# A decoder step with single-neuron experts: both f16 parts of a gate weight in one matmul of 256 columns for 88 of 256 tokens

## The chip, the cores and the metric

The kernel runs on one core of a Trainium2 chip. The metric is the device time of one execution in microseconds (us). Five engines work side by side, each through its own queue in order: TensorE (PE, with its weight loads shown apart as PEld), VectorE (DVE), ScalarE (ACT), GpSimd (POOL) and SyncE (SP). DMA transfers are started from the queues of SP, ACT and POOL.

## What is computed

The reference is one decoder layer for 256 prompt tokens and 64 sample tokens with a model width of 2048: attention and a gating unit, then a PEER layer, then a per-layer embedding. Only the PEER layer matters here. For each token it scores 128 + 128 keys in 8 heads, takes the best 16 pairs of each head, and so names 8 x 16 = 128 experts out of 128 x 128 = 16384, each a single neuron:

```python
v1, i1 = lax.top_k(s1, PEER_TOPK)
v2, i2 = lax.top_k(s2, PEER_TOPK)
sc, ci = lax.top_k(cand, PEER_TOPK)      # cand: all sums of v1 and v2
e = take(i1, ci // PEER_TOPK) * N_KEYS + take(i2, ci % PEER_TOPK)
```

The token's result is the sum over its 128 experts e of g(e) * gelu(x . u(e)) * v(e), where g is the softmax of the scores within a head, and u and v are the experts' rows.

## The kernel before

For the 256 prompt tokens the kernel does not gather rows of experts. It computes all 16384 experts densely, and multiplies each hidden value by a gate that is zero where the expert was not chosen. An expert's number is (row, column) in a 128 x 128 grid. The dense work is cut into 128 hidden units of 128 experts: `u_unit(e)` multiplies the unit's weights with the tokens (three passes for F32R precision, L94 to L96 in `mm3`, 48 matmuls of 256 columns into the PSUM tile `ps_mm`), and ACT applies gelu (L647). Each weight tile comes by an SP DMA as f32 and is split in halves: ACT makes the high part `w_hi` (L77), DVE the low part `w_lo` (L78), in a ring of four buffers. Later units (L639, L640) use 512 and 256 columns. `v_group(g)` then takes eight units at a time, and sums over them into `ps_o` (again L94 to L96), from where DVE adds to the residual `hT` (L813), 256 times in all.

The gates are built between units 14 and 28 by `g_batch(tb)`, sixteen calls of sixteen tokens, each in two halves of NB = 8 tokens. For a half, DVE makes with f16 tiles of 128 partitions (the token's 128 choices) and 1024 columns: `e1` and `e2`, the one-hot rows and columns of the choices (L704), and `p1`, `p2`, which are `e1` times the high and the low f16 part of the gate weight (L706). The weight is scaled by WSC = 16384 ahead of the split. The columns lie as 128 keys x 4 tokens, so one token's 128 columns have a stride of four elements. For each token PE multiplies `e2` (as the weights) by `p1` and by `p2`, both accumulated into the same 128 columns of a PSUM tile `ps_s` (L711): this gives the token's 128 x 128 grid of gates. Four tokens (a quad) fill one tile; there are two buffers of it. ACT copies the quad with the scale 1/WSC into `g_st` (L715), in which a token's values lie with a stride of 16 f32 elements. After 16 tokens a POOL DMA writes `g_st` to the DRAM matrix `gd` (L721).

`weights(g)` reads a group's gates back by an ACT DMA (`g_t`, L782), DVE multiplies the hidden values by them (L786), and ACT and DVE split the product (`wh` L114, `wl` L117) for `v_group`. The first group cannot start before the last batch of gates has gone through `gd`.

The order on each engine is not written by hand here: a scheduler interleaves the batches with the units ahead of time, and the queues then run in that order. Before the change a batch stands on PE as sixteen f16 matmuls, 7 of a hidden unit, sixteen f16 matmuls, 41 of hidden units.

Of the kernel before, what the change touches and what calls it, by code (L numbers as in the profile page):

```python
# [15 lines left out]
F16 = mybir.dt.float16  # L16
AF = mybir.ActivationFunctionType
ALU = mybir.AluOpType
AX = mybir.AxisListType

P = 128
D = 2048
NC_ = D // P
TP = 256
# [15 lines left out]
WSC = 16384.0  # L40
# [8 lines left out]
def _build(ctx, tc, nc, a):  # L49
    vec, act, pool, pe = nc.vector, nc.scalar, nc.gpsimd, nc.tensor  # L50
# [15 lines left out]
    def psum(tag, cols, parts=P):  # L66
        t = ps.tile([P, 512], F32, tag=tag, name="ps_" + tag)
        return t[:parts, :cols]
# [18 lines left out]
    def unit(src, lo_eng=None):  # L87
        r = raw.tile([P, 16, P], F32, name="w_raw")
        nc.sync.dma_start(r.rearrange("p a b -> p (a b)"), src)
        return split(r, lo_eng)  # L90

    def mm3(out, w, xh, xl, start, stop):
        wh, wl = w
        pe.matmul(out, wh, xh, start=start, stop=False)  # L94
        pe.matmul(out, wh, xl, start=False, stop=False)  # L95
        pe.matmul(out, wl, xh, start=False, stop=stop)  # L96
# [58 lines left out]
    hT = cp.tile([P, NC_, T], F32, name="hT")  # L155
# [108 lines left out]
    for b4 in range(2):  # L264
        pt = psum("tr", 512)
# [188 lines left out]
    for h in range(SH):  # L454
        tok = toks[h]
        for i in range(3):
            n = P if i < 2 else TS
# [6 lines left out]
        for sl, n, b in ((slice(0, TP), 2, bias[:, h]), (slice(TP, T), DB, bias[:, h, 0:DS])):  # L464
# [5 lines left out]
                op0=ALU.mult, op1=ALU.add,  # L470
# [20 lines left out]
    with tc.tile_pool(name="wo", bufs=2, reuse_waits="tile") as wo:  # L491

        early = [psum(tag, T) for tag in ("mm", "mm", "o", "o")]
        for half in range(2):
            for o2 in range(2):
                w = unit(a["w_out"][2 * half + o2])
                for k in range(2):
                    for c in range(8):
                        i = 8 * half + c
                        mm3(early[2 * o2 + k], w(8 * k + c), *xmix(i), i == 0, i == NC_ - 1)  # L500
        for o in range(NC_):
            xr = wo.tile([P, T], F32, name="xr", bufs=4)
            pool.dma_start(xr, a["xT"][o])
            if o < 4:
                pt = early[o]
            else:
                pt = psum("mm", T)
# [100 lines left out]
    for n, h in enumerate((0, 4, 1, 5, 2, 6, 3, 7)):  # L608
        sp = [psum("s", 256), psum("tr", 256), psum("o", 256)]
        r0 = 64 * (h // 4)  # L610
        for half in range(2):
            pt = psum("mm", T)
            dense(pt, unit(a["wq"][2 * h + half]), xh)
            q = rt.tile([P, T], F32, name="q_t", bufs=2)
# [5 lines left out]
        for i in range(2):  # L620
# [3 lines left out]
            scale=rcol[r0 : r0 + 64, 2:3],  # L624
# [5 lines left out]
    def u_unit(e, halves):  # L630

        t = up.tile([P, TP], F32, name="act", bufs=LEAD)
        w = unit(a["uT"][e])
        x = lambda c: (A0 if c < 8 else C)[2][:, c % 8, :, 0:TP]
        if halves:
            pt = psum("mm", 2 * TP).rearrange("p (a t) -> p a t", a=2)
            for c in range(NC_):
                wh, wl = w(c)
                pe.matmul(pt, wh, x(c), start=c == 0, stop=False)  # L639
                pe.matmul(pt[:, 0], wl, x(c)[:, 0], start=False, stop=c == NC_ - 1)  # L640
            act.activation(t, pt[:, 1], AF.Copy)
            vec.tensor_add(t, t, pt[:, 0])
        else:
            pt = psum("mm", TP)
            for c in range(NC_):
                mm3(pt, w(c), x(c)[:, 0], x(c)[:, 1], c == 0, c == NC_ - 1)
        act.activation(t, t if halves else pt, AF.Gelu_apprx_tanh)  # L647
        acts[e] = t
# [33 lines left out]
    NB = 8  # L682
    with tc.tile_pool(name="oh", bufs=2, side="right", reuse_waits="tile") as ohp:
        i4 = ohp.tile([P, NK, 4], F16, name="i4", bufs=1)
        vec.tensor_copy(i4, i128.unsqueeze(2).to_broadcast([P, NK, 4]))

        small = [ohp.tile([P, 4, P], F16, name=f"sel{i}", bufs=1) for i in range(2)]
        for tp, b in zip(picks, small):
            act.activation(b[:, 0:2], tp[:, 0 : 2 * P].rearrange("p (a b) -> p a b", a=2), AF.Copy)
            act.activation(b[:, 2], tp[:, 2 * P :], AF.Copy, scale=WSC)  # L690
            vec.scalar_tensor_tensor(b[:, 3], tp[:, 2 * P :], WSC, b[:, 2], op0=ALU.mult, op1=ALU.subtract)

        def g_batch(tb):
            st = ohp.tile([P, NK, 16], F32, name="g_st")
            for hb in range(16 // NB):
                t0 = tb * 16 + hb * NB
                t1 = t0 % P
                shape = [P, NB // 4, NK, 4]
                of = lambda k: (
                    small[t0 // P][:, k, t1 : t1 + NB].rearrange("p (q t) -> p q t", t=4).unsqueeze(2).to_broadcast(shape)  # L700
                )
                e1, e2, *parts = [ohp.tile(shape, F16, name=n) for n in ("e1", "e2", "p1", "p2")]
                for k, e in enumerate((e1, e2)):
                    vec.tensor_tensor(e, i4.unsqueeze(1).to_broadcast(shape), of(k), op=ALU.is_equal)  # L704
                for k, p in enumerate(parts):
                    vec.tensor_mul(p, e1, of(2 + k))  # L706
                for q in range(NB // 4):
                    gp = psum("s", 512)
                    for t in range(4):
                        for k, p in enumerate(parts):  # L710
                            pe.matmul(  # L711
                                gp[:, t * P : t * P + P], e2[:, q, :, t], p[:, q, :, t], start=k == 0, stop=k == 1
                            )
                    b = hb * NB + 4 * q
                    act.activation(  # L715
                        st[:, :, b : b + 4].rearrange("p a t -> p t a"),
                        gp.rearrange("p (t a) -> p t a", t=4),
                        AF.Copy,
                        scale=1.0 / WSC,
                    )  # L720
            pool.dma_start(  # L721
                gd[:, :, tb * P : tb * P + P].rearrange("g p x -> p g x"),
                st.rearrange("p (g i) t -> p g (i t)", g=NG),
            )


        for c4 in range(4):
            tp = psum("tr", 512)
            for c in range(4 * c4, 4 * c4 + 4):
                xd = ohp.tile([P, 2, TS], F32, name="xd", bufs=4)  # L730
                act.activation(
                    xd, hT[:, c, TP:].unsqueeze(1).to_broadcast([P, 2, TS]), AF.Copy, scale=g_ffn[:, c : c + 1]
                )
                pe.transpose(tp[:, c % 4 * P : c % 4 * P + P], xd.rearrange("p a b -> p (a b)"), ident)
            act.activation(xc[:, c4 * 512 : c4 * 512 + 512], tp, AF.Copy)

        tb = 0
        for e in range(AHEAD, U1):
            u_unit(e, False)
            while tb < 16 and tb * (U1 - AHEAD) < 16 * (e - AHEAD + 1):  # L740
                g_batch(tb)
                tb += 1
# [32 lines left out]
    def paced():  # L775
        state["unit"] += 1
        while state["n"] < min(128, state["unit"] * 128 // N_UNITS):
            c_step()
# [15 lines left out]
    def add_samples():  # L794
        for c4 in range(2):
            pt = psum("tr", 512)
            for c in range(8):
                dt = 8 * c4 + c
                pe.matmul(pt[:, c * TS : c * TS + TS], acc[:, dt * P : dt * P + P], stack, start=True, stop=True)
            vec.tensor_add(  # L800
                hT[:, 8 * c4 : 8 * c4 + 8, TP:], hT[:, 8 * c4 : 8 * c4 + 8, TP:],
                pt.rearrange("p (c t) -> p c t", c=8),
            )

    def v_group(g, ws):
        for d2 in range(8):
            w = unit(a["v_t"][g, d2])
            for k in range(2):
                pt = psum("o", TP)
                for i in range(GRP):  # L810
                    mm3(pt, w(8 * k + i), *ws[i], i == 0, i == GRP - 1)
                dt = 2 * d2 + k
                vec.tensor_add(hT[:, dt, 0:TP], hT[:, dt, 0:TP], pt)  # L813
            paced()
            if g == NG - 1 and d2 == 1:
                add_samples()
# [6 lines left out]
    for g in range(NG):  # L823
        v_group(g, ws)
        if g + 1 < NG:
            upto = LEAD + (NK - LEAD) * (g + 1) // (NG - 1)
            while done < upto:
                if done == upto - 1 and upto < NK:
                    ws = weights(g + 1)
                u_unit(done, True)  # L830
                paced()
                done += 1
            if upto == NK:
                ws = weights(g + 1)
# [5 lines left out]
    with tc.tile_pool(name="pl", bufs=2, reuse_waits="tile") as pl:  # L840
# [5 lines left out]
        for o in range(NC_):  # L846
            if o % 8 == 0:
                w_ple = unit(a["ple_w"][o // 8])
            pp = psum("s", T)
# [9 lines left out]
        for o in range(NC_):  # L859
            pt = psum("mm", T)  # L860
# [130 lines left out]
```

## Time and profile before

| | us |
|---|---|
| median of 3 runs | 2167.61 |
| lowest and highest run | 2167.24, 2169.64 |
| the profiled execution | 2168.27 |
| its span in the profile | 2166.5 |
| PE busy in the span | 2151.7 (99%) |
| DVE busy | 1699.5 (78%) |
| ACT busy | 1034.0 (48%) |
| POOL busy | 254.8 (12%) |

The span is the time from the first to the last instruction that the profile holds; the profiled execution took 1.8 us more. Records of matmuls overlap, since they are pipelined: what one costs on PE is the distance from its start to the next one's, not its duration.

### The profile page before, as it was taken

What the parts mean: (1) busy time and instruction counts of PE and PEld (TensorE: products, weight loads), DVE (VectorE), ACT (ScalarE), POOL (GpSimd) and SP (SyncE); (2) the same over time, 40 slices, a digit from 0 to 9 for tenths busy, and PEclk for the clock granted to TensorE, in tenths of its full rate; (3) what the DMA queues carried; (4) which work ended last, traced back from release to release, by engine and by line L of the source; (5) the groups of instructions that cost most, each with busy time, mean ns of one, the idle gap of its engine ahead of it and who ended that gap; (6) DMA issues with size and microseconds to landing.
All of it is one profiled execution on the core that took longest, in us unless ns stands there. A gap on an engine that the chain in (4) does not pass through costs nothing.

```text
span 2166.5 us, 38217 instructions
## 1 busy us (share of the span) xinstructions
PE 2151.7 (99%) x15552; PEld 2040.7 (94%) x15552; DVE 1699.5 (78%) x2808; ACT 1034.0 (48%) x1544; POOL 254.8 (12%) x190
## 2 busy tenths in 40 slices
PE   8999999999999999999999999999999999999999
PEld 7879999999999999999999999999999999999998
DVE  6674875799988688788878888788888888788754
ACT  5346454335476644444444444444444444445632
POOL 2000000000001111111111111111212221111000
PEclk9999999999999999999999999999999999999999
DMA  7412354343567788888788878889888888887452
GB/s 278 142 59 99 121 187 162 134 137 137 173 197 235 223 322 328 307 315 315 296 321 316 306 291 317 305 311 330 292 311 310 309 312 317 297 317 250 169 180 83
DMA packets 80575, 531.39 MB, mean 245 GB/s; under 512 B 9126, under 2 KB 13654, under 8 KB 19584
## 3 DMA queue, kind: packets, MB, share of 16 engines
q1 hardware_dynamic: 49936, 349.76, 45.3%
q0 software_dynamic: 24912, 158.30, 19.7%
q10 hardware_dynamic: 5552, 20.91, 2.6%
q8 instruction: 122, 2.00, 0.4%
q14 instruction: 53, 0.43, 0.1%
HBM read 509.07 MB, written 20.84 MB: 245 GB/s over the span
## 4 chain that ended last, share of the span: by engine, by line
PE 90%; issue 5%; DVE 2%; DMA 1%; ACT 1%; POOL 1%; ACTq 0%; SPq 0%; POOLq 0%; DVEq 0%
PE ps_mm L639 16%; PE ps_o L94 11%; PE ps_o L96 11%; PE ps_o L95 11%; PE ps_mm L95 9%; PE ps_mm L94 9%; PE ps_mm L96 8%; PE ps_mm L640 8%; PE ps_s L711 1%; POOL gd L721 1%; DVE w_lo L78 1%; DMA hT<-in_xT 0%; DMA g_t<-gd 0%; PE ps_s L94 0%; PE ps_s L96 0%
## 5 line engine op out<-in xcount | busy, mean ns | idle before, releaser
L77 ACT ACTIVATE w_hi<-w_raw 128x1024 fp32r<-128x1024 f32 x662 | 700.8, 1059 | 921.9 <-PE ps_o L95 340.2
L78 DVE TENSOR_TENSOR w_lo<-w_raw,w_hi 128x1024 fp32r<-128x1024 f32 x662 | 805.9, 1222 | 249.0 <-ACT w_hi L77 244.9
L94 PE MATMUL ps_o<-wh,w_hi 128*128 128x256 f32 x2048 | 575.5, 281 | 0.8 <-ACT wh L114 0.8
L95 PE MATMUL ps_o<-wl,w_hi 128*128 128x256 f32 x2048 | 573.3, 280 | 1.0 <-DVE wl L117 1.0
L96 PE MATMUL ps_o<-wh,w_lo 128*128 128x256 f32 x2048 | 569.9, 278 | 0.3 <-DVE w_lo L78 0.3
L95 PEld LDWEIGHTS ps_o<-wl,w_hi 128*128 128x128 f32 x2048 | 385.0, 188 | 1.4 <-DVE wl L117 1.4
L94 PEld LDWEIGHTS ps_o<-wh,w_hi 128*128 128x128 f32 x2048 | 384.4, 188 | 1.8 <-ACT wh L114 1.2
L96 PEld LDWEIGHTS ps_o<-wh,w_lo 128*128 128x128 f32 x2048 | 385.0, 188 | 0.5 <-DVE w_lo L78 0.5
L95 PE MATMUL ps_mm<-a,w_hi 128*128 128x320 f32 (+1 forms) x1008 | 310.5, 308 | 1.2 <-DVE a L119 1.2
L94 PE MATMUL ps_mm<-a,w_hi 128*128 128x320 f32 (+1 forms) x1008 | 308.7, 306 | 1.5 <-ACT w_hi L187 1.1
L96 PE MATMUL ps_mm<-a,w_lo 128*128 128x320 f32 (+1 forms) x1008 | 306.8, 304 | 0.5 <-DVE w_lo L78 0.3
L639 PE MATMUL ps_mm<-a,w_hi 128*128 128x512 f32 x768 | 270.9, 392 | 0.0
L639 PE MATMUL ps_mm<-c,w_hi 128*128 128x512 f32 x768 | 270.8, 391 | 0.0
L640 PE MATMUL ps_mm<-c,w_lo 128*128 128x256 f32 x768 | 215.1, 280 | 0.0
L640 PE MATMUL ps_mm<-a,w_lo 128*128 128x256 f32 x768 | 215.1, 280 | 0.0
L95 PEld LDWEIGHTS ps_mm<-a,w_hi 128*128 128x128 f32 x1008 | 190.5, 189 | 9.0 <-issue 6.6
L94 PEld LDWEIGHTS ps_mm<-a,w_hi 128*128 128x128 f32 x1008 | 190.3, 189 | 8.2 <-issue 4.9
L96 PEld LDWEIGHTS ps_mm<-a,w_lo 128*128 128x128 f32 x1008 | 190.3, 189 | 4.4 <-issue 3.2
L639 PEld LDWEIGHTS ps_mm<-c,w_hi 128*128 128x128 f32 x768 | 143.7, 187 | 31.8
L639 PEld LDWEIGHTS ps_mm<-a,w_hi 128*128 128x128 f32 x768 | 143.7, 187 | 31.3
L757 POOL DMA_INDIRECT row<-in_v_rows,c_e x64 | 111.3, 1739 | 496.2 <-DVE xc L770 444.6
L757 POOL DMA_INDIRECT row<-in_u_rows,c_e x64 | 100.7, 1573 | 510.7 <-DVE row L762 504.5
(343 smaller groups left out, 3145.3 us busy)
## 6 DMA issues: line engine op xcount, KB each, us to landing
w_raw<-in_uT SPq DMA_DIRECT2D x128, 1024.0 KB, 5.0
w_raw<-in_v_t SPq DMA_DIRECT2D x128, 1024.0 KB, 6.6
w_raw<-in_w_in SPq DMA_DIRECT2D x25, 1024.0 KB, 4.9
w_raw<-in_w_out SPq DMA_DIRECT2D x16, 1024.0 KB, 4.8
w_raw<-in_wq SPq DMA_DIRECT2D x16, 1024.0 KB, 4.8
gd<-g_st POOLq DMA_DIRECT2D x16, 1024.0 KB, 6.3
g_t<-gd ACTq DMA_DIRECT2D x16, 1024.0 KB, 6.2
w_raw<-in_w_gate SPq DMA_DIRECT2D x16, 1024.0 KB, 5.0
```

The costliest lines, as they stand in the source:

```text
L77: last = act.activation(hi, s, AF.Copy)
L78: (lo_eng or vec).tensor_sub(lo, s, hi.bitcast(F32))
L94: pe.matmul(out, wh, xh, start=start, stop=False)
L95: pe.matmul(out, wh, xl, start=False, stop=False)
L96: pe.matmul(out, wl, xh, start=False, stop=stop)
L639: pe.matmul(pt, wh, x(c), start=c == 0, stop=False)
L640: pe.matmul(pt[:, 0], wl, x(c)[:, 0], start=False, stop=c == NC_ - 1)
L711: pe.matmul(gp[:, t * P : t * P + P], e2[:, q, :, t], p[:, q, :, t], start=k == 0, stop=k == 1)
L721: pool.dma_start(gd[:, :, tb * P : tb * P + P].rearrange("g p x -> p g x"), st.rearrange("p (g i) t -> p g (i t)", g=NG),)
L757: pool.indirect_dma_start(out=row, out_offset=None, in_=tab, in_offset=bass.IndirectOffsetOnAxis(ap=c_e[:, j : j + 1], axis=0),)
```

## The change

`p1` and `p2` become the two halves of one tile `pp`. A quad is made in a new way when its number (4 * tb + b // 4) is a multiple of three: 22 of the 64 quads, 88 of the 256 tokens. For two such tokens one `ps_s` tile is taken, and for each token one matmul of 256 columns (128 for each part) fills half of it (L715 of the changed kernel). ACT copies the high parts' 128 x 2 x 128 values to `g_st` (L717), and DVE adds the low parts' from PSUM onto them there (L718). The other quads are made as before (L723, L726), without the scale. 1/WSC is applied later instead: the 256 additions into `hT` become `scalar_tensor_tensor` instructions (L823).

On PE this takes away 88 matmuls and 88 weight loads, and 88 of the remaining ones have 256 columns. ACT has 42 copies of 128 x 512 and 44 of 128 x 2 x 128 in place of 64 of 128 x 512. DVE has 44 additions more. The numbers of instructions on POOL and SP are the same.

```diff
-                e1, e2, *parts = [ohp.tile(shape, F16, name=n) for n in ("e1", "e2", "p1", "p2")]
+                e1, e2 = [ohp.tile(shape, F16, name=n) for n in ("e1", "e2")]
+                pp = ohp.tile([P, 2] + shape[1:], F16, name="pp")
...
-                for k, p in enumerate(parts):
-                    vec.tensor_mul(p, e1, of(2 + k))
+                for k in range(2):
+                    vec.tensor_mul(pp[:, k], e1, of(2 + k))
                 for q in range(NB // 4):
+                    b = hb * NB + 4 * q
+                    if (4 * tb + b // 4) % 3 == 0:
+
+                        for t in range(0, 4, 2):
+                            gp = psum("s", 512).rearrange("p (t k a) -> p t k a", t=2, k=2)
+                            for i in range(2):
+                                pe.matmul(gp[:, i], e2[:, q, :, t + i], pp[:, :, q, :, t + i], start=True, stop=True)
+                            o = st[:, :, b + t : b + t + 2].rearrange("p a t -> p t a")
+                            act.activation(o, gp[:, :, 0], AF.Copy)
+                            vec.tensor_add(o, o, gp[:, :, 1])
+                        continue
                     gp = psum("s", 512)
                     for t in range(4):
-                        for k, p in enumerate(parts):
+                        for k in range(2):
                             pe.matmul(
-                                gp[:, t * P : t * P + P], e2[:, q, :, t], p[:, q, :, t], start=k == 0, stop=k == 1
+                                gp[:, t * P : t * P + P], e2[:, q, :, t], pp[:, k, q, :, t], start=k == 0, stop=k == 1
                             )
...
                         AF.Copy,
-                        scale=1.0 / WSC,
                     )
...
-                vec.tensor_add(hT[:, dt, 0:TP], hT[:, dt, 0:TP], pt)
+                vec.scalar_tensor_tensor(
+                    hT[:, dt, 0:TP], pt, 1.0 / WSC, hT[:, dt, 0:TP], op0=ALU.mult, op1=ALU.add
+                )
```

The scheduler's order changes with it. After the change a pattern of three batches (twelve quads) repeats. In the order of PE, with "a" to "k" for the four fast quads a, c, g, j and the eight slow ones b1, b2, d1, d2, h1, i1, k1, k2, and "F n" for n matmuls of hidden units, it reads: F 35, a, F 14, b1, b2, F 2, c1, F 2, c2, F 29, d1, d2, F 6, g1, F 2, g2, F 5, h1, F 37, i1, j1, F 5, j2, F 7, k1, k2. A fast quad's two pairs are c1 and c2.

PE before, the end of a half-batch in the middle of the stage (`e_...` is the column one-hot as weights, `p_...` the two products, `a_78` the tokens' high or low part):

```order
L711 LDWEIGHTS e_8003
L711 MATMUL ps_s<-p_8004,e_8003 128x128
L711 LDWEIGHTS e_8003
L711 MATMUL ps_s<-p_8005,e_8003 128x128
L95 MATMUL ps_mm<-a_78,w_hi 128x256
L96 MATMUL ps_mm<-a_78,w_lo 128x256
L94 MATMUL ps_mm<-a_78,w_hi 128x256
```

PE after, at such a place, the quad b2's end and the fast quad c:

```order
L723 LDWEIGHTS e_7978
L723 MATMUL ps_s<-pp,e_7978 128x128
L94 MATMUL ps_mm<-a_78,w_hi 128x256
L95 MATMUL ps_mm<-a_78,w_hi 128x256
L715 LDWEIGHTS e_7978
L715 MATMUL ps_s<-pp,e_7978 128x256
L715 LDWEIGHTS e_7978
L715 MATMUL ps_s<-pp,e_7978 128x256
L96 MATMUL ps_mm<-a_78,w_lo 128x256
L94 MATMUL ps_mm<-a_78,w_hi 128x256
L715 LDWEIGHTS e_7978
L715 MATMUL ps_s<-pp,e_7978 128x256
```

The run of sixteen f16 matmuls is broken up: behind b2 two matmuls of a hidden unit, the first pair, two more, the second pair.

DVE before, one batch between two splits of weight halves:

```order
L78 TENSOR_TENSOR w_lo<-w_raw,w_hi 128x1024 x2
L704 TENSOR_TENSOR e_7975<-i_6479,sel_6482 128x1024
L706 TENSOR_TENSOR p_7976<-e_7974,sel_6482 128x1024
L706 TENSOR_TENSOR p_7977<-e_7974,sel_6482 128x1024
L704 TENSOR_TENSOR e_8003<-i_6479,sel_6482 128x1024
L706 TENSOR_TENSOR p_8004<-e_8002,sel_6482 128x1024
L706 TENSOR_TENSOR p_8005<-e_8002,sel_6482 128x1024
L704 TENSOR_TENSOR e_8093<-i_6479,sel_6482 128x1024
```

DVE after, where the additions of two fast quads, a and c, fall:

```order
L78 TENSOR_TENSOR w_lo<-w_raw,w_hi 128x1024 x2
L718 TENSOR_TENSOR g_st<-g_st,ps_s 128x2x128 x2
L705 TENSOR_TENSOR e_8067<-i_6479,sel_6482 128x1024
L705 TENSOR_TENSOR e_8068<-i_6479,sel_6482 128x1024
L707 TENSOR_TENSOR pp<-e_8067,sel_6482 128x1024
L718 TENSOR_TENSOR g_st<-g_st,ps_s 128x2x128
L707 TENSOR_TENSOR pp<-e_8067,sel_6482 128x1024
L718 TENSOR_TENSOR g_st<-g_st,ps_s 128x2x128
L705 TENSOR_TENSOR e_8094<-i_6479,sel_6482 128x1024
```

The additions of one quad stand behind the two splits `w_lo`, those of the next between the products of a later half-batch.

## Rows read from the trace of the kernel before

**Rows 1.** Page: busy us, share of span, instructions, by engine.

```profile
PE 2151.7 (99%) x15552; PEld 2040.7 (94%) x15552; DVE 1699.5 (78%) x2808; ACT 1034.0 (48%) x1544; POOL 254.8 (12%) x190
```

**Rows 2.** Windows: stretch, length, each engine's busy us (instructions), clock, DMA share, GB/s.

```profile
612.00:754.00 142.00, 142.00 (x1193) 139.79 (x1192) 107.63 (x148) 97.09 (x109) 17.34 (x15) 1.00 0.70 221
...
760.00:780.00 20.00, 17.89 (x141) 16.88 (x141) 12.35 (x26) 9.62 (x17) 2.42 (x2) 1.00 0.85 321
```

**Rows 3.** Groups by line and form, 605 to 757 us: busy us, mean ns, idle before.

```profile
L715 ACT ACTIVATE g_st<-ps_s 128x512 f32<-128x512 f32 x64 | 64.5, 1092 | 9.6 <-PE ps_s L711 9.6
L711 PEld LDWEIGHTS <-e 128*128 128x128 f16 x512 | 55.9, 117 | 2.2
```

**Rows 4.** Timeline of PE, 681.2 to 684.4 us: start, duration, instruction.

```profile
681.40 2.07 PE L711 MATMUL ps_s<-p,e 128*128 128x128 f16 x16
683.22 0.37 PE L94 MATMUL ps_mm<-a,w_hi 128*128 128x256 f32 x1
...
684.14 0.53 PE L711 MATMUL ps_s<-p,e 128*128 128x128 f16 x3
```

**Rows 5.** Timeline of PEld, a weight load that stands alone.

```profile
618.69 0.11 PEld L711 LDWEIGHTS <-e 128*128 128x128 f16 x1
```

**Rows 6.** Timeline of PE, the matmul that follows it.

```profile
618.84 0.27 PE L711 MATMUL ps_s<-p,e 128*128 128x128 f16 x1
```

**Rows 7.** Groups by line and form, the whole span: matmuls by width, one load.

```profile
L94 PE MATMUL ps_o<-wh,w_hi 128*128 128x256 f32 x2048 | 575.5, 281 | 0.8 <-ACT wh L114 0.8
L94 PE MATMUL ps_mm<-c,w_hi 128*128 128x320 f32 x256 | 79.1, 309 | 0.0
L639 PE MATMUL ps_mm<-c,w_hi 128*128 128x512 f32 x768 | 270.8, 391 | 0.0
L94 PEld LDWEIGHTS ps_o<-wh,w_hi 128*128 128x128 f32 x2048 | 384.4, 188 | 1.8 <-ACT wh L114 1.2
```

**Rows 8.** Timeline of PE, later units, 512 and 256 columns in turn.

```profile
999.79 0.39 PE L639 MATMUL ps_mm<-a,w_hi 128*128 128x512 f32 x1
1000.02 0.28 PE L640 MATMUL ps_mm<-a,w_lo 128*128 128x256 f32 x1
1000.14 0.39 PE L639 MATMUL ps_mm<-a,w_hi 128*128 128x512 f32 x1
```

**Rows 9.** Groups by line and form, the whole span: contiguous copies and additions.

```profile
L735 ACT ACTIVATE xc<-ps_tr 128x512 f32<-128x512 f32 x4 | 2.4, 610 | 0.0
L641 ACT ACTIVATE act<-ps_mm 128x256 f32<-128x256 f32 x96 | 35.1, 365 | 9.4 <-PE ps_mm L640 9.4
L813 DVE TENSOR_TENSOR hT<-hT,ps_o 128x256 f32<-128x256 f32 x256 | 107.0, 418 | 68.5 <-PE ps_o L96 67.3
L653 DVE SCALAR_TENSOR_TENSOR xt<-hT,c_gains,rs_y 128x256 f32<-128x256 f32 x16 | 6.8, 478 | 0.0
```

**Rows 10.** Timeline of ACT, 676 to 690 us, idle time before in brackets.

```profile
681.48 1.06 ACT L77 ACTIVATE w_hi<-w_raw 128x1024 fp32r<-128x1024 f32 x1 [1.82 <-PE ps_mm L95]
682.45 0.37 ACT L647 ACTIVATE act<-ps_mm 128x256 f32<-128x256 f32 x1
682.71 2.00 ACT L715 ACTIVATE g_st<-ps_s 128x512 f32<-128x512 f32 x2
685.29 2.03 ACT L715 ACTIVATE g_st<-ps_s 128x512 f32<-128x512 f32 x2 [0.58 <-PE ps_s L711]
```

**Rows 11.** The chain that ended last, 748 to 775 us, two of its pieces.

```profile
754.44 6.08 DMA gd<-g_st
...
760.59 8.32 DMA g_t<-gd
```

**Rows 12.** Timeline of PE, 768.9 to 776.9 us, where the gates come back.

```profile
769.07 0.28 PE L96 MATMUL ps_mm<-c,w_lo 128*128 128x256 f32 x1
769.87 0.39 PE L94 MATMUL ps_o<-wh,w_hi 128*128 128x256 f32 x1 [0.52 <-ACT wh L114]
```

More of the change, by code (lines that the diff above doesn't have):

```diff
@@ L701, in g_batch @@
                 )
-                e1, e2, *parts = [ohp.tile(shape, F16, name=n) for n in ("e1", "e2", "p1", "p2")]
+                e1, e2 = [ohp.tile(shape, F16, name=n) for n in ("e1", "e2")]
+                pp = ohp.tile([P, 2] + shape[1:], F16, name="pp")
                 for k, e in enumerate((e1, e2)):
                     vec.tensor_tensor(e, i4.unsqueeze(1).to_broadcast(shape), of(k), op=ALU.is_equal)
-                for k, p in enumerate(parts):
-                    vec.tensor_mul(p, e1, of(2 + k))
+                for k in range(2):
+                    vec.tensor_mul(pp[:, k], e1, of(2 + k))
                 for q in range(NB // 4):
+                    b = hb * NB + 4 * q
[8 more added lines that the diff above has]
+                        continue
                     gp = psum("s", 512)
                     for t in range(4):
-                        for k, p in enumerate(parts):
+                        for k in range(2):
                             pe.matmul(
-                                gp[:, t * P : t * P + P], e2[:, q, :, t], p[:, q, :, t], start=k == 0, stop=k == 1
+                                gp[:, t * P : t * P + P], e2[:, q, :, t], pp[:, k, q, :, t], start=k == 0, stop=k == 1
                             )
-                    b = hb * NB + 4 * q
                     act.activation(
```

## The prediction

> **What bounds the kernel now.** I read the page first, then the stretch of the stage that the change touches, then its groups of instructions, then single stretches of PE, ACT and DVE. The page shows PE busy for 99% of the span, DVE for 78%, ACT for 48% [rows 1]. From 612 to 754 us, where the gate batches run between the hidden units, PE is busy all 142 us at a granted clock of 1.00 (the 2.4 GHz level), DVE 107.63 us, ACT 97.09 us [rows 2]. So here nothing but PE's own time, or a wait put in its way, moves the end. In that stretch 1193 matmuls start, one each 119 ns; a batch of 16 tokens is 32 + 48 = 80 matmuls, 9.52 us, and three batches, after which the new pattern repeats, 28.57 us. DVE has 107.63/142 of that, 21.7 us, and ACT 19.5 us. The one place where PE does stand still is behind the stage: 17.89 us busy of 20 between 760 and 780 us [rows 2], while the matrix of gates goes to DRAM (6.08 us) and the first group of it comes back (8.32 us) [rows 11]; the matmuls that wait for it begin at 769.87 [rows 12].
>
> **The matmul, the term that decides the sign.** A fast token trades two matmuls of 128 f16 columns for one of 256. What the trace shows of the old ones: sixteen in a row start in 681.40 to 683.22, 114 ns each, with the next matmul delayed to about 118 each when the 0.9 us to the next run are shared out [rows 4]. A 256-column F32R matmul takes the same 117 ns start to start, and a 512-column one 230 ns [rows 8]. So an f16 matmul of half the columns costs PE as much as an F32R one. Two readings explain this. The first: its columns pass at half the rate. For F32R the records of 256, 320 and 512 columns last 281, 309 and 391 ns [rows 7]: 0.43 ns a column and 171 ns beside it. A lone f16 matmul, whose weights were in by 618.80 [rows 5], lasts 0.27 us [rows 6], so (270-171)/128 = 0.8 ns a column. By it 256 f16 columns cost as much as 512 F32R ones, 230 ns, against 2 x 118: saved 6 to 8 ns a token, over the 88 fast tokens 0.6 us. The second: the load of the 128 x 128 weights sets the pace, since its record lasts 117 ns, the very spacing [rows 3]; then 256 columns cost one spacing, and 88 x 118 ns = 10.4 us are saved. Since loads overlap matmuls, and F32R loads have longer records, 188 ns [rows 7], at the same spacing, I take the first, and keep the second as a bound and a rival. The Trainium skill's page TensorE: Matmul & The Clock Gate, section Back-to-back issue gap, gives the gap as about the number of columns at 2.4 GHz; here the f16 run shows twice that for 128 columns [rows 4], and the page would price the new matmul at about 109 ns (an estimate from it), near the second reading.
>
> The fast pairs are cut into more runs among the F32R matmuls. A switch costs some 0.09 us in and out: 7 F32R matmuls from 683.22 take 0.92 us to the next f16 one, where 7 x 0.118 = 0.83 [rows 4]. The order has about five more switches in three batches, but most of the 0.09 us is already what a run of eight has at its own end; between 0 and 0.5 us a period, taken as nil beside the waits below, kept in the range (up to 2.5 us).
>
> **The evacuation.** Before: one ACT copy of 128 x 512 with a write of stride 16, 1092 ns, 64 times [rows 3]. A contiguous copy of that shape takes 610 ns [rows 9], so the stride costs 0.94 ns an element. A fast quad needs two copies of 256 elements (365 ns contiguous [rows 9] + 0.24 = 0.60 us each), 1.2 us against 1.09, in all 22 x 0.12 = 2.6 us of ACT, hidden (ACT has 45 us free in the stage). New on DVE are 44 adds of 256 elements from PSUM onto the strided tile. Contiguous, such an add takes 418 ns [rows 9]; with the strided write's price from ACT, 0.66 us (taken); with reading and writing each paying it, 0.9 to 0.95; lower bound 0.42. That is 18 to 42 us of DVE, 29 taken. Eight adds fall in three batches: DVE goes from 21.7 to at most 21.7 + 8 x 0.66 = 27.0 us, still under PE's 28.6. The Trainium skill's page SBUF — State Buffer, section Door 1, says that a stride of up to 4 fp32 is free and a longer one pays on every line; the copy of 1092 against 610 ns agrees with it. The same rule would make the f16 columns at stride 4 free, which the 0.27 us of [rows 6] speaks against.
>
> **The waits that it adds.** The tiles in PSUM that take these products come from two buffers, before and after. A slow quad occupies one through eight matmuls and one copy; a fast pair through two matmuls, a copy and an add, and then it hands the buffer on. So each of the fast matmuls comes 0.5 us after the quad ahead of it, and finds that quad's copy (1.05 us behind a start some 0.2 us after its last matmul) still running. Reference times: in the run of sixteen from 681.40, ACT first ends a w_hi (681.48, 1.06 us) and an activation, and begins the two copies at 682.71, which end at 684.71; where ACT is free it begins at 685.29, 0.21 us after the eighth matmul from 684.14 [rows 4, 10]. In three batches there are four fast quads:
> - a, first of its half-batch behind 35 F32R matmuls: no wait for itself. Its copies end some 1.0 and 1.5 us after its matmuls, but the adds stand on DVE behind two w_lo, so the first ends near 2.1 us, and the second quad, wanted after 14 F32R matmuls at 1.7 us, waits 0.4 us.
> - c, behind two slow quads b1 and b2 and two F32R matmuls. From b1's start: copies end at about 2.25 and 3.2 us. c1 is wanted at 1.9 + 0.3 = 2.2, c2 at 2.2 + 0.5 + 0.3 = 3.0: together 0.3 to 0.5 us, taken 0.4.
> - g, behind d1, d2 and six F32R matmuls, with w_hi and the activation ahead of d1's copy: copies end at 2.4 and 3.35 us, g1 is wanted at 2.7 and g2 at 3.5; the next slow quad h1 at 4.6, when g1's add has just ended. 0 to 0.4 us, taken 0.15.
> - j: j1 comes right behind i1's eight, j2 at 2.1 us from i1's start, while i1's copy, behind w_hi and the activation, ends at 2.45. 0.35 to 0.6 us, taken 0.4.
> Sum 1.35 us in three batches, or about 0.34 a fast quad, x 22 quads = 7.4 us. With an add of 0.42 us it is some 0.7 us a period (3.9 us), with 0.95 us about 2.5 (13.8 us). PE has no slack in the stage to take these in: behind each waiting f16 matmul stand all later F32R matmuls of the hidden units. On DVE, behind an add that waits for its copy, stand the next masks, which are made half a batch ahead, and w_lo.
>
> **The stage's end.** The last product quad is now a fast pair, so the DMA of the last gates waits for a copy and an add in place of a copy (0.60 + 0.66 against 1.09: +0.2 us). By the order 125 F32R matmuls lie between it and the first that needs the returned gates, where there were 137: 12 x 0.118 = 1.4 us less to cover the 14.4 us of [rows 11]. Against this the weights of the first group are split somewhat earlier, which takes about 0.5 us from what PE lost at 769 to 776. Net +0.4 to +1.9, taken +1.2 us. The order moves nothing on SP and POOL; gd on POOL only starts by the add in place of the copy.
>
> **The scale.** The 256 additions into hT become one instruction with a scale: 418 ns before; a similar one with a scalar per partition takes 478 [rows 9], so 0 to 15 us on DVE, spread over 1250 us in which PE is busy 99% and DVE has a fifth free. At nothing, under PE's matmuls; were DVE late there, it would be up to 15 us. The f16 masks and products on DVE are the same in number.
>
> **Sum.** -0.6 + 7.4 + 1.2 = +8.0 us on the profiled execution's 2168.3 us (its span 2166.5 and 1.8 around it), which lies 0.7 above the median of the runs shown: 2176.3, said 2176.
>
> **The rivals.**
> - The 256-column matmul costs one spacing. For it: the load's 117 ns [rows 3]. Against it: the lone record [rows 6]. PE gains 10.4 us, but reaches each wanted buffer up to 0.2 us earlier, so that the waits grow by some 2 to 3 us: -10.4 + 10 + 1.2 = +1, between 2163 and 2171. The break-even is a saving of about 99 ns a token; the new matmul would have to cost 137 ns or less.
> - The strided add is dear and DVE becomes the bound of the stage: from 0.87 us an add, eight of them fill the 6.9 us that DVE has free in three batches. At 0.95 the waits of 13.8 us and 5.3 periods x 0.7 us give 2183 to 2188. For it: the add reads and writes the strided tile, and no row shows such an instruction. Against it: the strided write alone explains ACT's row.
> - The change does nothing that can be seen: copies end sooner than I count, because ACT, whose w_hi now wait on later matmuls, is free at those points; the waits and the saving are both under 2 us: 2166 to 2170.
>
> **How the numbers follow.** Forecast (matmul at double cost, waits exposed) 0.50, 2171 to 2182; cheap matmul 0.22; DVE the bound 0.13; nothing seen 0.15. The range leaves out the far ends of the cheap-matmul and DVE cases: 2165 to 2185. A measurement of this kernel can tell about 0.2%, 4.3 us, from no change, that is 2163.3 to 2171.9. Faster than that only the cheap matmul with covered waits, 0.10. The same: the rest of that case, all of the third, and the low end of the forecast, 0.34. Slower: 0.56.
>
> **What would show it.** In the profile after: two 256-column f16 matmuls start to start, 230 ns (the forecast) or about 118; the add's mean duration, 0.66 or up to 0.95; between 612 and 754 us idle time of PE in front of the f16 matmuls, ended by the ACT copy of a slow quad (c, j) or the DVE add (behind a), near 0.3 us a fast quad; DVE at about 27 us in three batches; the first matmul on the returned gates about 1 us later against the last F32R one of the hidden units. A wait of PE for w_lo rather than for PSUM would show the waits wrong; so would PE with no idle time in the stage and the kernel at 2168.

## The result, and the profile after

The changed kernel takes 2180.7 us (median of 6 runs), the one before 2168.3 beside it: 1.0058 times as long, with a 95% interval of 1.0047 to 1.0068. It is slower by 12.4 us; the forecast was 2176, slower, with a range of 2165 to 2185. The profiled execution has a span of 2178.2 us, 11.7 more than before. One execution of a kernel told of below took 2952.7 us at a mean granted clock of 0.65, and no ratio here counts it.

The page of the kernel after, busy us by engine:

```profile
PE 2160.2 (99%) x15464; PEld 2039.7 (94%) x15464; DVE 1723.5 (79%) x2852; ACT 1036.8 (48%) x1566; POOL 254.4 (12%) x190
```

Against [rows 1] PE has 88 matmuls less and is "busy" 8.5 us more. Most of PE's waiting does not show as idle time, because the matmul that started last is still in its pipeline while the next one waits. DVE has 44 instructions and 24 us more.

Groups of the kernel after by line and form, 605 to 775 us: busy us, mean ns of one, idle before:

```profile
L726 ACT ACTIVATE g_st<-ps_s 128x512 f32<-128x512 f32 x42 | 43.0, 1091 | 22.3 <-PE ps_s L723 22.3
L718 DVE TENSOR_TENSOR g_st<-g_st,ps_s 128x256 f32<-128x256 f32 x44 | 27.1, 632 | 19.9 <-ACT g_st L717 19.6
L717 ACT ACTIVATE g_st<-ps_s 128x256 f32<-128x256 f32 x44 | 26.7, 642 | 3.7 <-PE ps_s L715 3.6
L715 PE MATMUL ps_s<-pp,e 128*128 128x256 f16 x88 | 26.4, 401 | 1.5 <-ACT g_st L726 0.6
```

The strided addition lasts 632 ns (0.66 was taken), the copy of 256 elements 642 (0.60), the copy of 512 as long as in [rows 3]. The record of the 256-column f16 matmul, 401 ns, is that of a 512-column F32R one, 391 [rows 7].

Timeline of PE in the kernel after around a fast quad c (start, duration, instruction):

```profile
653.34 0.37 PE L94 MATMUL ps_mm<-a,w_hi 128*128 128x256 f32 x1
653.54 0.28 PE L95 MATMUL ps_mm<-a,w_hi 128*128 128x256 f32 x1
653.97 0.62 PE L715 MATMUL ps_s<-pp,e 128*128 128x256 f16 x2
654.23 0.48 PE L96 MATMUL ps_mm<-a,w_lo 128*128 128x256 f32 x1
654.54 0.28 PE L94 MATMUL ps_mm<-a,w_hi 128*128 128x256 f32 x1
654.85 0.61 PE L715 MATMUL ps_s<-pp,e 128*128 128x256 f16 x2
655.11 0.48 PE L95 MATMUL ps_mm<-a,w_hi 128*128 128x256 f32 x1
655.43 0.28 PE L96 MATMUL ps_mm<-a,w_lo 128*128 128x256 f32 x1
```

and of ACT at the same time:

```profile
652.83 1.97 ACT L726 ACTIVATE g_st<-ps_s 128x512 f32<-128x512 f32 x2
654.62 0.61 ACT L717 ACTIVATE g_st<-ps_s 128x256 f32<-128x256 f32 x1
655.50 0.64 ACT L717 ACTIVATE g_st<-ps_s 128x256 f32<-128x256 f32 x1 [0.27 <-PE ps_s L715]
```

A matmul of 256 F32R columns starts 0.12 us after another. So the first fast pair was due at 653.66 and starts at 653.97, when the first of ACT's two copies (some 1.09 us from 652.83) has ended; the second was due at 654.66 and starts at 654.85, just after the second copy (654.80). Together 0.5 us; 0.4 was forecast for c. From the first pair's start to the second F32R start behind it (654.54) are 0.57 us: two wide matmuls of 230 ns and one F32R of 0.12, and nothing is lost.

How far each execution lies behind the one before, at the start of the same gelu on ACT (worked out from the traces; the column on the left is its time in the kernel before):

| before, us | after | after, second profile | fast pairs in buffers of their own |
|---|---|---|---|
| 603.2 (stage begins) | +4.5 | -0.2 | +1.8 |
| 644.3 | +8.3 | +3.1 | +2.7 |
| 653.9 | +8.8 | +3.7 | +2.9 |
| 663.4 | +9.3 | +4.2 | +2.9 |
| 758.7 (stage ends) | +12.8 | +7.8 | +2.6 |
| 854.6 | +11.7 | +10.0 | +5.4 |
| span | +11.7 | +10.6 | +5.0 |

The second and third column of differences belong to runs told below. The stage itself costs 8.3 and 7.9 us. What lies ahead of it in the first profile, 4.5 us, has nothing to do with the change.

### The profile page after: what moved, and what is told of

It reads as the page before. It is cut to its first block, busy times and chain, and to the rows that moved or that the text cites. A ratio compares the mean times of both kernels' runs of the same rounds, so it can differ in the third digit from the quotient of the medians.

```text
span 2178.2 us, 38112 instructions
## 1 busy us (share of the span) xinstructions
PE 2160.2 (99%) x15464; PEld 2039.7 (94%) x15464; DVE 1723.5 (79%) x2852; ACT 1036.8 (48%) x1566; POOL 254.4 (12%) x190
## 4 chain that ended last, share of the span: by engine, by line
PE 93%; DMA 2%; DVE 2%; ACT 1%; issue 1%; POOL 0%; SPq 0%; ACTq 0%; DVEq 0%; POOLq 0%
PE ps_mm L639 16%; PE ps_o L94 11%; PE ps_o L95 11%; PE ps_o L96 11%; PE ps_mm L95 10%; PE ps_mm L94 10%; PE ps_mm L96 10%; PE ps_mm L640 8%; PE ps_s L723 1%; DMA g_t<-gd 1%; PE ps_s L715 1%; ACT g_st L726 1%; DVE w_lo L78 1%; DMA hT<-in_xT 0%; PE ps_s L94 0%
## 5 line engine op out<-in xcount | busy, mean ns | idle before, releaser
L94 PEld LDWEIGHTS ps_mm<-a,w_hi 128*128 128x128 f32 x1008 | 191.4, 190 | 12.1 <-issue 4.9
L823 DVE SCALAR_TENSOR_TENSOR hT<-ps_o,hT 128x256 f32<-128x256 f32 x256 | 107.9, 422 | 67.4 <-PE ps_o L96 66.3
```

What stands on the lines that cost most here:

```text
L823: vec.scalar_tensor_tensor(hT[:, dt, 0:TP], pt, 1.0 / WSC, hT[:, dt, 0:TP], op0=ALU.mult, op1=ALU.add)
```

## Experiments: what PE waits for

**Fast pairs in PSUM buffers of their own.** The two buffers of tag "o" are idle in this stage.

```diff
-                            gp = psum("s", 512).rearrange("p (t k a) -> p t k a", t=2, k=2)
+                            gp = psum("o", 512).rearrange("p (t k a) -> p t k a", t=2, k=2)
```

> The changed kernel, but the fast pairs take their PSUM tiles from the two buffers that the second phase uses (tag o, idle in this stage) instead of sharing the two of the slow quads. The order of PE stays as it was but for a few rows. Theory (PE stands still because two buffers hand on too slowly): the waits of about 1.1 to 1.3 us in three batches vanish, PE's clock stays at its upper level throughout the stage, and the time is 2167 to 2171, with 256-column f16 matmuls still 230 ns apart. Rival (the pace of the changed kernel comes from ACT's or DVE's own queues, or from late w_lo): 2178 to 2182, with the idle time now in front of other instructions.

Measured: 2174.4 us (2173.8 for the executions in the ratio), 1.0024 times the kernel before (1.0015 to 1.0034). Neither expectation holds as it stood: half of the loss is gone. Its waits are read from a second profile.

> The same kernel as a_tag_o (fast pairs in two PSUM buffers of their own), for a profile of an execution at the full clock: the one taken first ran at a mean granted clock of 0.65. The time measured was 2174.4, half of the loss gone. Theory: in the profile no f16 matmul waits for a PSUM buffer any more, and what is left, about 5 us, lies in the fast pairs' DVE additions pushing back the masks or w_lo (PE waits for w_lo or products). Rival: what is left lies in the order itself, that is more switches between f16 and F32R runs, with PE never idle.

Measured: 2173.3 us, in one run. Windows of the stage: the kernel after first, then this one (length, busy us of each engine with instructions, clock, DMA share, GB/s):

```profile
612.00:766.00 154.00, 151.51 (x1141) 139.35 (x1139) 134.34 (x196) 102.03 (x140) 17.34 (x15) 0.99 0.64 200
```

```profile
612.00:757.00 145.00, 144.81 (x1125) 132.94 (x1124) 129.62 (x193) 99.09 (x134) 17.34 (x15) 1.00 0.63 205
```

The idle time of PE falls from 2.5 to 0.2 us. By the table above the stage costs 0.9 us where it cost 8.3 and 7.9: 1.1 are lost by 654 us, and from there to its end 0.26 are gained, in eleven batches with 59 fast tokens, 4.4 ns for each. (The windows differ by 9 us, since they are set by eye and the first begins 2.7 us earlier in its stage.) The additions on DVE are there as before, and DVE is busy 129.62 of 145 us, so they are not what PE waits for.

The run by itself does not part the buffers from the order, since the scheduler made another one for it: seven stretches of hidden-unit matmuls in three batches, where the changed kernel has eleven and the kernel before six. "But for a few rows" was wrong. The changed kernel's own trace parts them, here between 740 and 754 us (PE, then DVE, then ACT):

```profile
740.77 2.06 PE L723 MATMUL ps_s<-pp,e 128*128 128x128 f16 x16
...
743.39 0.62 PE L715 MATMUL ps_s<-pp,e 128*128 128x256 f16 x2
...
745.39 0.87 PE L723 MATMUL ps_s<-pp,e 128*128 128x128 f16 x6
...
753.26 0.61 PE L715 MATMUL ps_s<-pp,e 128*128 128x256 f16 x2
```

```profile
744.69 0.65 DVE L718 TENSOR_TENSOR g_st<-g_st,ps_s 128x256 f32<-128x256 f32 x1 [1.02 <-ACT g_st L717]
```

```profile
752.13 1.08 ACT L726 ACTIVATE g_st<-ps_s 128x512 f32<-128x512 f32 x1
```

A switch that waits for no buffer costs nothing: the sixteen products of d1 and d2 and the six hidden-unit matmuls behind them take 2.62 us (740.77 to 743.39), 0.119 each, as in [rows 2] with fewer switches. And each late start stands right behind the operation that hands its buffer back: h1 at 745.39 behind g1's addition (its end at 745.34), the second pair of j at 753.26 behind i1's copy (753.21). Both pairs of c, the second of g and the quad behind a also start 0.05 us behind a copy or an addition. So the waits are for the shared buffers.

What is left against the kernel before is 5.0 us of the span: 1.8 lie ahead of the stage, and some 3 behind it, which the account of the stage's end below takes up. No wait of PE for late masks or w_lo shows in the stage, so that expectation fell too.

**The changed kernel once more.**

> The changed kernel once more, for a second profile and more executions with their mean granted clocks. In the first profile 4.5 us of the 11.7 us that the span grew lay before 200 us, with a clock of 0.74 from 180 to 200 us, ahead of every changed instruction, and one dip to 0.65 lay within the stage at 644 to 648 us, where PE had waited 0.9 us. Theory (PE's waits in the stage make its clock fall there in some executions): again 2177 to 2184, with the stage's waits about 1.1 us in three batches where the clock is whole, and a dip inside the stage in this profile too. Rival (that dip was chance, as the one at 190 us): no dip inside the stage, and a span that is only 6 to 8 us over that of before.

Measured: 2180.0 us, 1.0055 (1.0038 to 1.0072), in four runs of 2178.9 to 2183.0. Windows of the first profile of the changed kernel:

```profile
180.00:200.00 20.00, 19.89 (x95) 16.44 (x96) 4.20 (x8) 10.10 (x51) 0.00 (x0) 0.74 0.15 52
...
644.00:648.00 4.00, 3.67 (x21) 3.31 (x21) 3.34 (x6) 2.19 (x4) 0.59 (x1) 0.65 0.64 185
```

and of the second:

```profile
180.00:200.00 20.00, 19.88 (x124) 16.99 (x125) 6.02 (x9) 10.24 (x48) 0.00 (x0) 1.00 0.28 94
612.00:764.00 152.00, 149.22 (x1127) 137.25 (x1126) 131.82 (x193) 99.96 (x131) 17.53 (x16) 1.00 0.66 205
776.00:780.00 4.00, 1.06 (x9) 0.84 (x8) 0.02 (x1) 0.00 (x0) 0.00 (x0) 1.00 1.01 426
780.00:784.00 4.00, 2.91 (x13) 2.72 (x14) 4.00 (x12) 3.56 (x9) 0.00 (x0) 0.66 0.76 320
```

From 180 to 200 us PE started 95 matmuls in the first and 124 in the second: there the clock was at its lower level (1.2 GHz) for part of the time in the one and not in the other, and 4.1 of the 4.5 us arise there (between 171 and 226 us). Within the stage the clock stayed whole in the second profile, and the stage cost 7.9 us all the same, against 8.3. So the waits cost what they cost by themselves; the theory that PE's waits pull the clock down within the stage is not borne out, and a dip there is worth about half a microsecond. Of the rival, the missing dip came true, but the span is 10.6 us over that of before and not 6 to 8. Behind the stage it is otherwise: PE stood still for most of 776 to 780 us, and from 780 to 784 the clock was 0.66.

## Experiments: what the wide matmul costs, and why

**The layout of the columns.** Masks and products as 128 keys x 2 tokens, not x 4, so that a token's f16 columns are 4 bytes apart and not 8; first in the kernel before:

```diff
-        i4 = ohp.tile([P, NK, 4], F16, name="i4", bufs=1)
+        i4 = ohp.tile([P, NK, 2], F16, name="i4", bufs=1)
...
-                shape = [P, NB // 4, NK, 4]
+                shape = [P, NB // 2, NK, 2]
...
-                                gp[:, t * P : t * P + P], e2[:, q, :, t], p[:, q, :, t], start=k == 0, stop=k == 1
+                                gp[:, t * P : t * P + P], e2[:, 2 * q + t // 2, :, t % 2], p[:, 2 * q + t // 2, :, t % 2], start=k == 0, stop=k == 1
```

> The kernel before with the masks and products laid out as 128 keys x 2 tokens in place of x 4, so that a token's f16 columns have a stride of two elements (4 bytes) and not four. Theory (the f16 columns pass at half the rate because of their stride): 128-column f16 matmuls start about 60 ns apart instead of 118; PE saves up to 512 x 58 ns = 30 us, but then waits for copies, so 2140 to 2165, if the 1024-column DVE operations stay near 0.69 us. Rival (the pace comes from the f16 weight load or from the type): spacing 118 ns and 2166 to 2170. If DVE slows with runs of two elements to over 1 us an operation, DVE bounds the stage and the time is above 2180.

Measured: 2156.1 us, 0.9938 (0.9922 to 0.9955). Timeline of PE in this kernel:

```profile
676.94 1.09 PE L711 MATMUL ps_s<-p,e 128*128 128x128 f16 x16
...
679.37 0.62 PE L711 MATMUL ps_s<-p,e 128*128 128x128 f16 x8 [0.46 <-DVE w_lo L78]
680.26 0.62 PE L711 MATMUL ps_s<-p,e 128*128 128x128 f16 x8 [0.28 <-ACT g_st L715]
```

Sixteen f16 matmuls now last 1.09 us from the first start to the last end, where they lasted 2.07 [rows 4]; their median distance is 57 ns, where it was 118. DVE's operations of 1024 columns stay at 0.69 us. More than half of PE's saving of some 30 us is given back (13 us are left): it now waits for the copies and for w_lo (the brackets).

The same layout in the changed kernel:

> The changed kernel with the same layout of 2 tokens. Theory (stride): the 256-column f16 matmul falls from 230 to about 118 ns, the 128-column one to 60; PE saves about 10 + 20 us, the waits for the two buffers grow, 2150 to 2175. Rival (weight load or type): spacings of 230 and 118 ns as before, 2178 to 2184.

Measured: 2166.1 us, 0.9990 (0.9980 to 0.9999). Two 256-column matmuls start 114 ns apart (median of 50 pairs), where it was 216 (208 to 235, but for one that waited), and 229 in the run where no pair waits for a buffer. Both are twice the price of 128 columns in the same layout. With the layout mended the changed kernel is still 10 us behind the kernel before with the same layout.

**Moving side or weights.** The products in the layout of 2, the one-hot `e2`, PE's weights, left in that of 4:

```diff
-                e1, e2, *parts = [ohp.tile(shape, F16, name=n) for n in ("e1", "e2", "p1", "p2")]
...
+                sh2 = [P, NB // 2, NK, 2]
...
+                e2 = ohp.tile(shape, F16, name="e2")
+                e1, *parts = [ohp.tile(sh2, F16, name=n) for n in ("e1", "p1", "p2")]
...
-                                gp[:, t * P : t * P + P], e2[:, q, :, t], p[:, q, :, t], start=k == 0, stop=k == 1
+                                gp[:, t * P : t * P + P], e2[:, q, :, t], p[:, 2 * q + t // 2, :, t % 2], start=k == 0, stop=k == 1
```

> The kernel before with the products (the moving operand) in the layout of 2 tokens and the one-hot e2 (the weights) still in that of 4. Theory (the moving columns' stride halves the pace): f16 matmuls 57 ns apart as in b_in2, weight loads still 117 ns long in the records. Rival (the stride of the weight load sets the pace): 118 ns apart.

Measured: 2158.5 us in one run. PE's timeline, and the weight loads of the stage from the groups:

```profile
676.35 1.14 PE L718 MATMUL ps_s<-p,e 128*128 128x128 f16 x16
...
L718 PEld LDWEIGHTS <-e 128*128 128x128 f16 x512 | 33.7, 114 | 14.6 <-issue 13.1
```

Sixteen in 1.14 us, a median of 60 ns apart, while the loads' records are still 114 ns long (97 with both sides in the layout of 2). So the pace of 118 came from the stride of the moving columns, and not from the load of the weights.

**The scale alone.** The kernel before with the scale taken from the copies and put into the additions into `hT`, and no other edit.

```diff
-                        scale=1.0 / WSC,
...
-                vec.tensor_add(hT[:, dt, 0:TP], hT[:, dt, 0:TP], pt)
+                vec.scalar_tensor_tensor(
+                    hT[:, dt, 0:TP], pt, 1.0 / WSC, hT[:, dt, 0:TP], op0=ALU.mult, op1=ALU.add
+                )
```

> The kernel before with nothing but the scale moved: the copies out of PSUM unscaled, the 256 additions into the residual as scalar_tensor_tensor with 1/WSC. Theory (hidden under PE): 2167 to 2170, the additions 0 to 60 ns longer each. Rival (DVE late in the second phase): up to 15 us more, 2175 to 2183.

Measured: 2170.4 us, 1.0006 (0.9997 to 1.0016). The group of these additions, whole span:

```profile
L812 DVE SCALAR_TENSOR_TENSOR hT<-ps_o,hT 128x256 f32<-128x256 f32 x256 | 107.8, 421 | 66.8 <-PE ps_o L96 66.0
```

421 ns against 418 [rows 9]: 0.8 us of DVE in all, out of sight.

## Experiments: a faster version, and the change on top of it

**Four buffers for the quads, with the layout of 2 tokens**, in the kernel before:

```diff
-                    gp = psum("s", 512)
+                    gp = psum("so"[q % 2], 512)
```

> The kernel before with the layout of 2 tokens (as b_in2) and four PSUM buffers for the quads: they alternate between the tags s and o. In b_in2 the f16 matmuls started 57 ns apart, but PE waited some 17 us in the stage, most of it for the two buffers that ACT's copies of 1.09 us give back. Theory (the two buffers are the limit): 2138 to 2150. Rival (ACT and DVE themselves are the limit once PE needs only 113 us of the stage): 2152 to 2158, with PE then waiting for w_lo and for products.

Measured: 2138.9 us, 0.9854 (0.9838 to 0.9871): 32 us faster than the kernel before beside it (2170.5), and 42 below the changed kernel's 2180.7. The stage's windows, of the layout alone and then with four buffers:

```profile
612.00:742.00 130.00, 118.75 (x1201) 114.13 (x1199) 108.09 (x150) 94.31 (x112) 17.35 (x15) 1.00 0.75 236
```

```profile
612.00:722.00 110.00, 110.00 (x1164) 109.05 (x1162) 105.19 (x148) 88.18 (x105) 17.34 (x15) 1.00 0.86 275
```

The windows do not hold quite the same work (1201 and 1164 matmuls); from the gelu at the stage's beginning to that behind its last batch it takes 125.6 us with four buffers and 142.7 with two, 17 less. PE has no idle time left in the window; DVE is busy for 105.19 of 110 us and stands next. Here too the order changed with the buffers: the scheduler puts a batch's 32 products in one run.

**The change with both cures.**

> The changed kernel with both cures: the layout of 2 tokens and PSUM buffers of their own (tag o) for the fast pairs. Theory (a matmul of 256 columns costs twice one of 128 in this layout too, 114 against 57 ns, so the change has nothing to give PE even when nothing stands in its way, and its 44 additions load DVE, which is full there): no faster than b_in2_so's 2139, 2141 to 2155. Rival (fewer instructions and weight loads help once the pace is 57 ns): 2130 to 2138.

Measured: 2162.5 us, 0.9968 (0.9955 to 0.9980): 24 us slower than the version without the change, more than expected. Its stage:

```profile
612.00:745.00 133.00, 122.33 (x1122) 113.31 (x1120) 127.39 (x191) 95.12 (x133) 17.35 (x15) 1.00 0.68 223
```

and what PE waited for in it (us in total, times, longest):

```profile
PE ps_s L723 <- DVE pp L707: 4.2, 10, 1.0
PE ps_mm L96 <- DVE w_lo L78: 1.9, 5, 0.7
```

DVE is busy 127.39 of 133 us, 25.4 of them with the additions: they make it the bound, and PE waits for masks and for w_lo. From gelu to gelu as above the stage takes 144.8 us, 19 more than without the change; most of the rest lies behind it, where the two transfers through DRAM took 17.6 us against 13.4. This is the rival of the prediction in which DVE takes over, in a kernel whose PE needs less than DVE.

**More cover for the stage's end.** The sixteen batches spread over 13 units.

```diff
-            while tb < 16 and tb * (U1 - AHEAD) < 16 * (e - AHEAD + 1):
+            while tb < 16 and tb * (U1 - AHEAD - 1) < 16 * (e - AHEAD + 1):
```

> b_in2_so with the sixteen batches of gates spread over 13 hidden units in place of 14, so that one unit more of PE work covers the way of the last gates through DRAM, where PE still lost about 4.7 us. Theory (the end of the stage is a fixed chain that needs cover): 2133 to 2137. Rival (DVE, which was busy 20 of 20 us from 620 to 660 us, cannot make the masks faster, and PE waits in the stage for what it gains at its end): 2138 to 2144.

Measured: 2142.9 us, 0.9878 (0.9860 to 0.9896), so the expected gain did not come. The time is that of the rival, but not its cause: from 612 to 715 us PE is idle 0.2 us. Two pieces of its chain of waits, start and us:

```profile
720.07 10.77 DMA gd<-g_st
730.91 4.72 DMA g_t<-gd
```

The last gates left earlier, but took 10.77 us to DRAM in this execution, where [rows 11] show 6.08; why, one profile does not tell. What it cost is one wait of PE, from 737 us on (total, times, longest), and DVE shows why the hidden units in between were no cover:

```profile
PE ps_mm L96 <- DVE w_lo L78: 5.2, 1, 5.2
```

```profile
735.66 1.09 DVE L786 TENSOR_TENSOR act<-act,g_t 128x256 f32<-128x256 f32 x3 [1.97 <-DMA g_t<-gd]
...
741.03 4.63 DVE L78 TENSOR_TENSOR w_lo<-w_raw,w_hi 128x1024 fp32r<-128x1024 f32 x4
```

In DVE's order the products with the returned gates stand ahead of the split of the next `w_lo`, so a hidden unit that could have run in the meantime waits for the gates as well.

## Why the prediction was right, point by point

**The bound, the wide matmul and the scale** came out as put down. PE's own waits set the end of the stage. The 256-column f16 matmul costs 230 ns and not 118, the break-even lay near 137, and so the rival with the cheap matmul is out: even at half the stride a wide one costs 114 against 57. The rival with DVE as the bound needed 0.87 us an addition, and it lasts 0.63. The first of the two readings of [rows 4 to 6] was right, and the runs name its cause, the stride. The saving of 0.6 us came out smaller: the kernel with buffers of its own gained 0.26 us in eleven of sixteen batches, 0.4 for the whole.

**The waits for the two buffers**, taken at 7.4 us, are nearly the whole of the stage's loss: 8.3 and 7.9 us, which fall to 0.9 with buffers of their own and the order that goes with them. Their rate was nearly right. Start of the quad a in the kernel after, one pattern apart (PE), and the kernel before's w_hi seven batches behind that of [rows 10] (ACT):

```profile
730.96 1.08 PE L715 MATMUL ps_s<-pp,e 128*128 128x256 f16 x4
...
760.64 1.09 PE L715 MATMUL ps_s<-pp,e 128*128 128x256 f16 x4
```

```profile
748.21 1.06 ACT L77 ACTIVATE w_hi<-w_raw 128x1024 fp32r<-128x1024 f32 x1 [1.82 <-PE ps_mm L95]
```

Before, a batch takes (748.21 - 681.48)/7 = 9.53 us, three 28.60; after, 29.68. That is 1.08 more, or 1.2 of waits less the saving of 0.1, where 1.35 and 0.1 were put down. c was 0.4 to 0.5, as forecast; a, behind 13 or 14 matmuls, loses only 0.1 in this part and not 0.4; g and the quad behind it 0.3 and not 0.15; j 0.4, as put down. What the sum missed is the start of the stage: the first four batches lose 3.8 and 3.3 us (the table from 603 to 644), where the steady rate gives 1.4. The prediction carried the steady order's waits over to all 22 quads, but there the order is another: behind a quad a stand four hidden-unit matmuls and not 14, and the slow quad behind them waits for a's addition:

```profile
639.29 1.09 PE L715 MATMUL ps_s<-pp,e 128*128 128x256 f16 x4
640.02 0.48 PE L94 MATMUL ps_mm<-a,w_hi 128*128 128x256 f32 x1
...
641.89 1.39 PE L723 MATMUL ps_s<-pp,e 128*128 128x128 f16 x10 [0.63 <-DVE g_st L718]
```

From 640.02 to 641.89 are 1.87 us, where four matmuls take 0.47: 1.4 us are lost, and as much at the same place in the second profile.

**The stage's end** was taken at +1.2 us (0.4 to 1.9). It came out as -1.2 in the first and +2.3 in the second profile, from 758.7 to 854.6 us of the table. The step that failed is that the way through DRAM was taken as of fixed length. Pieces of the chain of waits in the kernel after, first and second profile:

```profile
768.89 6.30 DMA gd<-g_st
775.27 6.91 DMA g_t<-gd
```

```profile
763.82 6.43 DMA gd<-g_st
770.33 9.63 DMA g_t<-gd
```

13.2 and 16.1 us, against 14.4 in [rows 11]. In the second profile PE waits for the first product with the returned gates (us in total, times, longest):

```profile
PE ps_o L94 <- ACT wh L114: 3.9, 1, 3.9
```

With fewer F32R matmuls to cover it the longer way leaves PE idle, and the clock falls on top (0.66 from 780 to 784 us). So the term is a range of -1 to +3 us, wider than the one given. The kernel with buffers of its own pays it too, 2.8 us, with 7.44 and 9.45 us for the two transfers: this is more than half of the 5 us that it kept. Whether the change makes the way longer stays open: in the profiles of five kernels without it (before, the scale alone, the layout of 2, four buffers, and 13 units) the two took 13.4 to 15.5 us together, in five profiles with it 13.2 to 17.6.

**The rest.** The sum of what the second profile shows is 7.9 + 2.8 - 0.2, its 10.6 us (the 2.8 counts to the end of the span), where 8.0 was forecast: the stage is 1.1 above its terms of 7.4 and -0.6, its end 1.6 above 1.2. The medians are 12.4 and 12.1 us apart, and the other 2 us go with the clock, which the sum has no term for. At the same mean granted clock the recorded executions of the two kernels are 9 to 10 us apart: at 0.998 the medians are 2169.9 (ten executions) and 2179.9 (two), at 0.997 2171.3 (seven) and 2180.5 (three). But the ten executions of the changed kernel have a mean of 0.9969, and 41 of the kernel before one of 0.9985; within each kernel an execution is some 1.4 us longer for each 0.001 less, so that is about 2 us (an estimate from these executions). The stretch at 0.66 behind the stage is one such fall; the profile of the kernel before has none from 755 to 870 us. What else makes them more frequent with the change stays open.

That the range held the result is in part luck: its upper end was put down for a longer addition and for switches (up to 2.5 us), and neither came; the clock, the longer way through DRAM and the start of the stage took that room.

## What to carry to other kernels

Price a matmul by the distance between starts for its own type and stride: a merge of two into a wider one gains only if the distance was set by something other than the columns. A product that passes the PSUM buffers in half the time needs the buffers back in half the time: with two of them, count when the copies ahead end before breaking a row of long fillings into short ones. And where an engine is close behind the bound, as DVE was here, a step moved onto it is free only as long as nobody makes the bound faster. Where a scheduler makes the order, a change of buffers is a change of order as well: compare the two orders before the buffers get the credit.

## What the hardware showed that was not expected

The pace of PE's moving operand depends on the stride of its columns: 128 f16 columns 8 bytes apart start 118 ns after one another, 4 bytes apart 57 ns, the pace of the F32R columns (256 in some 118 ns). The stride of the weights made little difference (60 ns with weights at 8 bytes). The Trainium skill's page SBUF — State Buffer, section Door 1, gives a stride of up to 8 bf16 as free. For the moving operand, here f16 of the same two bytes, these runs show otherwise, already at a stride of four. The strided addition on DVE, which reads and writes the strided tile, lasts 632 ns against 418 contiguous, no more than ACT pays for the strided write alone (642 against 365).
